# FoX queries and keys projected token-major and turned by DMA, with runs of 32 tokens, and conditioning columns listed and paced anew

## The chip, the cores and the metric

The program runs on one core of a Trainium2 chip. The metric is the device time of one execution in microseconds (us); lower is better. Besides the time there is one profiled execution, with every instruction's start and end on each engine: PE (TensorE matmuls), PEld (its weight loads), DVE (VectorE), ACT (ScalarE), POOL (GpSimd) and SP (which here only issues DMAs).

## The reference

Two decoder layers over 256 tokens of width 2048, float32. Each layer is a token mixer and a SwiGLU feed-forward (FFN), both behind an RMS norm whose scale and shift, as well as the gate of the residual, come from a conditioning vector `c` through `ada_w` (six vectors of 2048 for a layer). Layer 0 mixes with an mLSTM, layer 1 with "forgetting attention" (FoX):

```python
cs = silu(c)
for layer in range(2):
    sh1, sc1, g1, sh2, sc2, g2 = split(cs @ ada_w[layer] + ada_b[layer], 6)
    h = rms_norm(x, norm_mix_w[layer]) * (1 + sc1) + sh1
    y = mlstm_mixer(h, ...) if layer == 0 else fox_mixer(h, ...)
    x = x + g1 * y
    h = rms_norm(x, norm_ffn_w[layer]) * (1 + sc2) + sh2
    g, u = split(h @ w_gate_up[layer], 2)            # 2048 -> 2 * 5632
    x = x + g2 * ((silu(g) * u) @ w_down[layer])     # 5632 -> 2048
return rms_norm(x, final_norm_w)

def fox_mixer(h, w_in, b_f, w_out):                  # 16 heads of 128
    q, k, v, fl = split(h @ w_in, [D, 2 * D, 3 * D])
    cum = cumsum(log_sigmoid(fl + b_f), over tokens)
    s = q @ k.T * 128 ** -0.5 + cum[t] - cum[s]      # for each head, causal
    return (softmax(s) @ v) @ w_out
```

## The kernel before

Every big product is computed in three matmuls from two parts of each operand: a weight tile of 1 MB (`raw`, four slices k of 128 rows, 512 columns) is fetched by SP, ACT rounds it to `hi` (L261), DVE subtracts to get `lo` (L262), and PE multiplies. The activations stand transposed, hidden units on partitions: `hT[:, k]` holds 256 tokens as high parts and then the same 256 as low parts; `y` and `acts` are kept alike.

There are two forms of a column group (512 columns, 16 slices k, four ticks of four slices).

- `group_a` holds the activations still (128 tokens) and streams the weights: for each k and each half of the tokens, high x hi, high x lo and low x hi, three matmuls of 512 columns (L288, L289, L290). Two banks take the result, tokens on partitions ("token-major").
- `group_b` holds the weights still and streams the activations: for each k and each of four blocks of 128 columns, hi against 512 (both parts of the 256 tokens; L271) and lo against 256 (L274). Four banks take the result, columns on partitions; `total` adds the two halves of a bank (ACT L368, DVE L370 or L372).

FoX's q and k need columns of a head on partitions, so `keep_t` makes them with `group_b`, eight column groups in turn: q and k of heads 0 to 3, 4 to 7, 8 to 11 and 12 to 15. All else goes through `group_a`. Where a token-major result has to be turned, PE does it (`turned`), or, in three of the four FFN halves, DVE and DMAs: `blocks` transposes blocks of 32x32 (L353) and writes them to DRAM (`aside`), `gather` reads them back with the partitions in order (L361), both on POOL's queue, and some ticks later `flip` copies from there (ACT L1171, DVE L1172). There the four blocks of 128 columns lie next to each other for each token, so the flip reads with a step of four elements.

A `tick` stands at the end of every four slices: it takes `adv` entries off a list of small steps (`steps`) and pays `rate` of a conditioning column. The heads are such steps: `scores` (L691, L696 and L1229 on PE, then DVE, ACT and DVE), `flip` (PE transposes L958, ACT), `mix` (L1261, L1264, ACT, DVE). A conditioning column is 128 outputs of `cs @ ada_w`: a fetch of 1 MB and one DVE multiply with a sum (L193). They are listed by `want` in the order in which they are computed, 192 in all; `need` makes those at once that a later stage finds missing. When the two gates g1 and g2 of a layer are complete, `grow` spreads them over all partitions (PE, ACT, then POOL's queue).

`bridge` leads from one stage to the next: it ends a residual (DVE L442, L443), forms the norm (ACT, DVE L487), turns it on PE (L498) and begins the next product. Its order on PE, DVE and ACT is written out by hand. Elsewhere the order of each engine's instructions is set when the program is built, by a scheduler that works on estimates; a buffer goes to whoever can have it first. Weights and conditioning columns share five buffers of 1 MB; there are four pairs of `hi` and `lo`, each for two slices, and 16 `slot`s of 512 KB.

Of the kernel before, what the change touches and what calls it, by code (L numbers as in the profile page):

```python
# [27 lines left out]
    r0=(0.75, 0.7, 0.8, 0.5), fr=0.66, r1=(0.3, 0.3, 0.3, 0.3))  # L28
# [3 lines left out]
def kernel(  # L32
# [211 lines left out]

    def tick(n, adv=1):
        drain(adv)
        grow_all()
        bg(n)
# [20 lines left out]
    def mm_b(ps, hi, lo, rhs, first, last):  # L269
        def big():  # L270
            nc.tensor.matmul(ps, hi, rhs, start=first, stop=last, skip_group_check=True)  # L271

        def little():
            nc.tensor.matmul(  # L274
                ps[:, T:], lo, rhs[:, :T], start=False, stop=False, skip_group_check=True
            )

        if last:
            little()
            big()  # L280
        else:
            big()
            little()

# [10 lines left out]

    def group_b(w, nk, c0, act, evac, bgn, adv=1):
        banks = [bank() for _ in range(4)]
        for k in range(0, nk, 4):
            ws = load_w(w, k, 4, c0)
            for m in range(4):  # L300
                cols = slice(m * P, (m + 1) * P)
                for j, (hi, lo) in enumerate(ws):
                    mm_b(
                        banks[m], hi[:, cols], lo[:, cols], act(k + j), k + j == 0, k + j == nk - 1
                    )
                if k + 4 == nk:
                    evac(m, banks[m])
            tick(bgn, adv)
# [43 lines left out]
    def blocks(dst, src, aside):  # L352
        nc.vector.transpose(  # L353
            dst.rearrange("p (j b m) -> p j m b", j=4, m=4),
# [4 lines left out]
    def gather(whole, aside):  # L359
        for j in range(4):  # L360
            nc.gpsimd.dma_start(  # L361
                whole[32 * j : 32 * j + 32].rearrange("a (g b) m -> a g (b m)", b=32),
# [3 lines left out]
    def total(ps, out, scale=None):  # L366
        b = t256()
        nc.scalar.activation(b, ps[:, T:], AF.Copy, scale=1.0 if scale is None else scale)  # L368
        if scale is None:
            nc.vector.tensor_tensor(out, ps[:, :T], b, op=ALU.add)  # L370
        else:
            nc.vector.scalar_tensor_tensor(  # L372
                out=out, in0=ps[:, :T], scalar=scale, in1=b, op0=ALU.mult, op1=ALU.add
            )
# [678 lines left out]

# [57 lines left out]
    def ffn(layer, begun, norm, rates, nsplit=0, srate=0.0, nxt=None):  # L1111
# [23 lines left out]
        if nsplit:  # L1135
            want(0, G2)
            want(1, SC1, SH1)
            want(1, G1)

        rate = rates[0]  # L1140

        def column(c0):
# [280 lines left out]
```

## Time and profile before

| | |
|---|---|
| time, median of 3 runs (lowest, highest) | 2282.02 us (2279.60, 2283.16) |
| time of the profiled execution, and its span | 2279.4 us, 2277.6 us |
| busy share of the span: PE, PEld, DVE, ACT, POOL | 99%, 81%, 73%, 50%, 3% |
| read from HBM, written | 628.44 MB, 10.52 MB; 281 GB/s over the span |
| granted clock of PE, mean | 0.999 |

A row of a group reads: line, engine, operation, output<-inputs, shapes, count | busy us, mean ns of one | idle time of the engine just before them and what ended it. A row of the timeline or of the chain begins with its start and its length in us. A row of a window gives the stretch, its length, then busy us and, in brackets, the count of instructions for each engine. The stages in the span: mLSTM and norm up to 435 us, the first FFN to 1143, FoX from 1143 to 1545 (its q and k columns from 1215 to 1316 and from 1346 to 1444, its output product to 1545), the second FFN to the end. Matmuls overlap in the pipeline, so their pace is read from starts, not from lengths.

### The profile page before, as it was taken

The numbers are of one execution on the slowest core, as the hardware profiler recorded it, in microseconds if no ns is written. First come the engines' busy times: TensorE is split into PE (matmuls) and PEld (weight loads), VectorE is DVE, ScalarE is ACT, GpSimd is POOL, SyncE is SP. The second block draws the span as 40 slices with busy tenths as digits, with TensorE's granted clock in tenths as the row PEclk, the third lists the DMA queues.
The fourth block names the chain that finished last, engine by engine and source line by source line (L and its number), as shares of the span: only waits on it lengthen the run. The fifth ranks groups of instructions, "written<-read, shape, count | busy, mean of one in ns | idle before, by whom it ended". The sixth has DMA issues, their size and how long they took to land.

```text
span 2277.6 us, 26530 instructions
## 1 busy us (share of the span) xinstructions
PE 2255.0 (99%) x10250; PEld 1848.2 (81%) x10250; DVE 1653.0 (73%) x1865; ACT 1139.6 (50%) x1493; POOL 71.2 (3%) x136
## 2 busy tenths in 40 slices
PE   8999999999999999999999999999999999999998
PEld 5877878888888888888888888887888888888886
DVE  7998789878887878875687777777665555555564
ACT  4778564555543344444555444455444443444443
POOL 1000000000000000100000000000100100010000
PEclk9999999999999999999999999999999999999999
DMA  9998989788888889996667877675777665566662
GB/s 394 371 369 321 353 307 354 283 338 334 325 335 330 326 335 349 360 350 219 217 238 288 299 273 277 250 274 189 271 276 255 221 204 189 201 223 219 206 233 98
DMA packets 93571, 640.69 MB, mean 281 GB/s; under 512 B 11443, under 2 KB 11891, under 8 KB 19077
## 3 DMA queue, kind: packets, MB, share of 16 engines
q1 hardware_dynamic: 86400, 617.79, 73.5%
q0 software_dynamic: 6896, 21.08, 3.1%
q8 instruction: 80, 1.31, 0.2%
q14 instruction: 47, 0.38, 0.0%
q10 hardware_dynamic: 148, 0.14, 0.0%
HBM read 628.44 MB, written 10.52 MB: 281 GB/s over the span
## 4 chain that ended last, share of the span: by engine, by line
PE 87%; DVE 5%; DMA 4%; ACT 2%; issue 1%; POOL 0%; SPq 0%; ACTq 0%; DVEq 0%; POOLq 0%
PE mm L289 25%; PE mm L290 25%; PE mm L288 25%; PE mm L271 5%; PE mm L274 3%; DMA ada<-in_ada_w_dram 3%; DVE lo L262 2%; DVE ada L193 2%; ACT hi L261 1%; DMA slot<-in_w_in_dram 1%; PE aux L1010 0%; PE aux L498 0%; PE aux L1229 0%; PE mm L569 0%; PE mm L565 0%
## 5 line engine op out<-in xcount | busy, mean ns | idle before, releaser
L262 DVE TENSOR_TENSOR lo<-raw,hi 128x1024 fp32r<-128x1024 f32 x764 | 924.2, 1221 | 470.8 <-ACT hi L261 469.5
L261 ACT CAST hi<-raw 128x1024 fp32r<-128x1024 f32 x764 | 796.9, 1054 | 870.7 <-PE mm L290 742.2
L289 PE MATMUL mm<-lo,hT 128*128 128x512 f32 x1846 | 720.3, 390 | 3.3 <-DVE lo L262 3.2
L290 PE MATMUL mm<-hi,hT 128*128 128x512 f32 x1846 | 719.8, 390 | 0.0
L288 PE MATMUL mm<-hi,hT 128*128 128x512 f32 x1846 | 719.1, 392 | 0.0
L193 DVE SCALAR_TENSOR_TENSOR ada<-ada,cs 128x2048 f32<-128x2048 f32 x192 | 438.7, 2285 | 55.7 <-DMA ada<-in_ada_w_dram 55.3
L289 PEld LDWEIGHTS mm<-lo,hT 128*128 128x128 f32 x1846 | 346.7, 188 | 78.5 <-DVE lo L262 7.4
L290 PEld LDWEIGHTS mm<-hi,hT 128*128 128x128 f32 x1846 | 346.5, 188 | 72.4 <-issue 0.5
L288 PEld LDWEIGHTS mm<-hi,hT 128*128 128x128 f32 x1846 | 346.5, 188 | 71.9 <-issue 0.5
L288 PE MATMUL mm<-hi,slot 128*128 128x512 f32 x960 | 375.0, 391 | 0.2 <-ACT slot L1043 0.2
L289 PE MATMUL mm<-lo,slot 128*128 128x512 f32 x960 | 374.2, 390 | 0.2 <-DVE lo L262 0.2
L290 PE MATMUL mm<-hi,slot 128*128 128x512 f32 x960 | 374.1, 390 | 0.0
L288 PEld LDWEIGHTS mm<-hi,slot 128*128 128x128 f32 x960 | 180.3, 188 | 38.0 <-ACT slot L1043 0.8
L290 PEld LDWEIGHTS mm<-hi,slot 128*128 128x128 f32 x960 | 180.2, 188 | 37.7 <-issue 0.7
L289 PEld LDWEIGHTS mm<-lo,slot 128*128 128x128 f32 x960 | 180.2, 188 | 37.5 <-DVE lo L262 0.6
L271 PE MATMUL mm<-hT,hi 128*128 128x512 f32 x512 | 181.5, 401 | 0.0
L274 PE MATMUL mm<-hT,lo 128*128 128x256 f32 x512 | 138.4, 281 | 0.4 <-DVE lo L262 0.4
L271 PEld LDWEIGHTS mm<-hT,hi 128*128 128x128 f32 x512 | 94.4, 188 | 19.6
L274 PEld LDWEIGHTS mm<-hT,lo 128*128 128x128 f32 x512 | 96.6, 189 | 4.1 <-DVE lo L262 1.1
L865 ACT ACTIVATE slot<-mm 128x512 f32<-128x512 f32 x78 | 45.3, 596 | 39.7 <-PE mm L290 37.9
L357 POOL DMA_DIRECT2D aside<-t x32 | 18.0, 562 | 1239.7 <-DVE t L353 1239.7
L1172 DVE TENSOR_TENSOR slot<-slot,slot 128x512 fp32r<-128x512 f32 x32 | 34.8, 1090 | 24.8 <-ACT slot L1171 24.8
(220 smaller groups left out, 1049.6 us busy)
## 6 DMA issues: line engine op xcount, KB each, us to landing
ada<-in_ada_w_dram SPq DMA_DIRECT2D x192, 1024.0 KB, 6.3
raw<-in_gate_up_dram SPq DMA_DIRECT2D x176, 1024.0 KB, 5.2
raw<-in_down_dram SPq DMA_DIRECT2D x88, 1024.0 KB, 4.9
raw<-in_fox_in_dram SPq DMA_DIRECT2D x48, 1024.0 KB, 4.9
raw<-in_w_in_dram SPq DMA_DIRECT2D x44, 1024.0 KB, 7.2
raw<-in_w_out_dram SPq DMA_DIRECT2D x16, 1024.0 KB, 5.8
raw<-in_fox_out_dram SPq DMA_DIRECT2D x16, 1024.0 KB, 4.9
aside<-t POOLq DMA_DIRECT2D x32, 256.0 KB, 2.5
```

Source lines behind the costliest of these rows:

```text
L193: nc.vector.scalar_tensor_tensor(out=raw, in0=raw, scalar=1.0, in1=cs, op0=ALU.mult, op1=ALU.mult, accum_out=acc[layer][:, j : j + 1],)
L261: nc.scalar.copy(hi, raw[:, j : j + 2, :])
L262: nc.vector.tensor_tensor(lo, raw[:, j : j + 2, :], hi.bitcast(F32), op=ALU.subtract)
L271: nc.tensor.matmul(ps, hi, rhs, start=first, stop=last, skip_group_check=True)
L274: nc.tensor.matmul(ps[:, T:], lo, rhs[:, :T], start=False, stop=False, skip_group_check=True)
L288: nc.tensor.matmul(ps, a, hi, start=first, stop=False, skip_group_check=True)
L289: nc.tensor.matmul(ps, a, lo, start=False, stop=False, skip_group_check=True)
L290: nc.tensor.matmul(ps, b, hi, start=False, stop=last, skip_group_check=True)
L357: nc.gpsimd.dma_start(aside, dst)
L865: nc.scalar.activation(SP[i][:, t, :], banks[t], func)
L1172: nc.vector.tensor_tensor(dst[:, :, T:], ps, dst[:, :, :T].bitcast(F32), op=ALU.subtract)
```

## The change

Five edits.

- `keep_t` for layer 1 computes q and k with `group_a`, copies the two banks out with ACT (scaled), and turns them with `blocks` and `gather`. The heads' scores read k where `gather` put it; q is copied once more (`begin`, four heads in one ACT copy), six ticks after k's column (four for the last group), and the heads' steps are listed one tick later by `timed`. Two heads run together: scores of both, flips of both, mixes of both, one kind for each tick, since `adv` is 2. The v column that stood before the third group of heads stands behind the fourth.
- `blocks`, `gather` and `tiles` lay a turned tile out in runs of 32 tokens instead of single elements, for the FFN's flips as well.
- Layer 1's `project_out` computes 12 of the 16 slices of its first two columns before the last heads' results are asked for.
- The columns of layer 1 for SC2, SH2 and G2 are listed behind those of layer 0, with G1 after SC2 and SH2.
- The rates are 0.65, 0.6 and 0.52 for the second half of the first FFN (gate and up, then down) and for FoX, instead of 0.8, 0.5 and 0.66. SP's queue now has 9 conditioning columns within the second down product of layer 0 instead of none, 24 instead of 30 within FoX's input columns, and 6 instead of 8 within its output product.

```diff
@@ -25,7 +25,7 @@
 NEG = -1e30
 QN = (6, 9)
 CFG = dict(first=4, pace=(1.0, 1.0, 1.0), n2=4, lr=(0.9, 0.9, 0.95, 1.0, 1.15), sr=0.95, nsplit=11,
-    r0=(0.75, 0.7, 0.8, 0.5), fr=0.66, r1=(0.3, 0.3, 0.3, 0.3))
+    r0=(0.75, 0.7, 0.65, 0.6), fr=0.52, r1=(0.3, 0.3, 0.3, 0.3))
 
 
 @with_exitstack
@@ -242,7 +242,13 @@
         for _ in range(len(steps) if n is None else min(n, len(steps))):
             steps.pop(0)()
 
+    clock = [0]
+    timed = []
+
     def tick(n, adv=1):
+        clock[0] += 1
+        while timed and timed[0][0] <= clock[0]:
+            timed.pop(0)[1]()
         drain(adv)
         grow_all()
         bg(n)
...
@@ -351,7 +327,7 @@
 
     def blocks(dst, src, aside):
         nc.vector.transpose(
-            dst.rearrange("p (j b m) -> p j m b", j=4, m=4),
+            dst.rearrange("p (j m b) -> p j m b", j=4, m=4),
             src.rearrange("p (m j b) -> p j m b", m=4, j=4),
         )
         nc.gpsimd.dma_start(aside, dst)
@@ -359,19 +335,12 @@
     def gather(whole, aside):
         for j in range(4):
             nc.gpsimd.dma_start(
-                whole[32 * j : 32 * j + 32].rearrange("a (g b) m -> a g (b m)", b=32),
+                whole[32 * j : 32 * j + 32].rearrange("a (g c) -> a g c", c=P),
                 aside.rearrange("t (i a) c -> a (t i) c", a=32)[:, :, j * P : (j + 1) * P],
             )
 
...
+    def tiles(whole):
+        return whole.rearrange("p (g m b) -> p m g b", m=4, b=32)
 
     def split_act(src, dst):
         nc.scalar.copy(dst[:, :T], src)
@@ -1051,6 +1020,8 @@
     def interleave(*lists):
         return [f for fs in zip(*lists) for f in fs]
 
+    LAND = 6
+
     def keep_t(c0, bgn, scale=None, adv=1, layer_w=0):
         if layer_w == 0:
             i = COLS.index(c0)
@@ -1064,9 +1035,15 @@
 
             steps.append(flip)
             return o
-        o = slot().rearrange("p (k t) -> p k t", t=T)
-        group_b(w, KT, c0, h_act, lambda m, ps: total(ps, o[:, m, :], scale), bgn, adv)
-        return o
+        banks = group_a(w, c0, h_act, bgn, adv)
+        whole = slot()
+        aside = dram.tile([2, P, 512], F32, tag="aside", name=nm("aside"))
+        for t in range(2):
+            own = t512()
+            nc.scalar.activation(own, banks[t], AF.Copy, scale=1.0 if scale is None else scale)
+            blocks(t512(), own, aside[t])
+        gather(whole, aside)
+        return tiles(whole)
 
     for i in range(1, 4):
         unit(i, start[i], KT, LR[0])
@@ -1092,9 +1069,16 @@
 
     def project_out(wo, res, bgn, adv, upto, norm, w2, heads):
         act = lambda k: act_tile(y, k)
+        first = {}
+        if upto == 12:
+            for i in range(2):
+                first[i] = group_a(wo, 512 * i, act, bgn, adv, kb=upto, more=True)
+            assert not timed
+            drain()
         for i in range(3):
             res.both(i, group_a(
-                wo, 512 * i, act, bgn, adv, before=lambda k: drain() if k >= upto else None
+                wo, 512 * i, act, bgn, adv, ka=upto if i in first else 0, banks=first.get(i),
+                before=lambda k: drain() if k >= upto else None,
             ))
         return bridge(wo, 0, KT, 1536, act, res, 3, norm, w2, heads)
 
@@ -1135,7 +1119,9 @@
         if nsplit:
             want(0, G2)
             want(1, SC1, SH1)
+            want(1, SC2, SH2)
             want(1, G1)
+            want(1, G2)
 
         rate = rates[0]
 
@@ -1156,7 +1142,7 @@
             first = len(acts)
             acts.extend([None, None])
             if lag:
-                whole = slot().rearrange("p (t m) -> p t m", m=4)
+                whole = slot()
                 aside = dram.tile([2, P, 512], F32, tag="aside", name=nm("aside"))
                 for t in range(2):
                     blocks(t512(), sg[:, t, :], aside[t])
@@ -1164,14 +1150,14 @@
 
             def flip(i):
                 acts[first + i] = dst = new_act()
+                hi, lo = dst[:, :, :T], dst[:, :, T:]
                 if lag:
-                    ps = whole[:, :, 2 * i : 2 * i + 2].rearrange("p t m -> p m t")
+                    ps = tiles(whole)[:, 2 * i : 2 * i + 2]
+                    hi, lo = (x.rearrange("p m (g b) -> p m g b", b=32) for x in (hi, lo))
                 else:
                     ps = turned(sg, i)
-                nc.scalar.copy(dst[:, :, :T], ps)
-                nc.vector.tensor_tensor(
-                    dst[:, :, T:], ps, dst[:, :, :T].bitcast(F32), op=ALU.subtract
-                )
+                nc.scalar.copy(hi, ps)
+                nc.vector.tensor_tensor(lo, ps, hi.bitcast(F32), op=ALU.subtract)
 
             steps.extend([lambda: None] * lag)
             steps.extend([lambda: flip(0), lambda: flip(1)])
@@ -1211,8 +1197,6 @@
 
 
     w = fox_in
-    want(1, SC2, SH2)
-    want(1, G2)
     f_raw = slot()[:, : KT * 16].rearrange("p (k c) -> p k c", c=16)
     nc.scalar.dma_start(f_raw, fox_gates)
     y = [None] * 8
@@ -1227,7 +1211,8 @@
             for t in range(2):
                 n = P * (t + 1)
                 nc.tensor.matmul(
-                    S[:, T * t : T * t + n], q[:, t * P : (t + 1) * P], k[:, :n],
+                    S[:, T * t : T * t + n].rearrange("p (g b) -> p g b", b=32),
+                    q[:, t * P : (t + 1) * P], k[:, : n // 32],
                     start=False, stop=t == 1, skip_group_check=True,
                 )
             mx = small([P, 2], "den", bufs=4)
@@ -1292,15 +1277,22 @@
     u3 = split3(cum, 16, new)
     for i in range(4):
         if i == 1:
-            vals[2] = keep_v(group_a(w, 2 * D + 1024, h_act, FR, ka=12, banks=begun[2 * D + 1024]))
-        if i == 2:
-            vals[3] = keep_v(group_a(w, 2 * D + 1536, h_act, FR, 2))
-        q = keep_t(512 * i, FR, P ** -0.5, layer_w=1)
-        k = keep_t(D + 512 * i, FR, layer_w=1)
-        drain()
-        steps.extend(interleave(*[
-            fox_head(4 * i + j, q[:, j, :], k[:, j, :]) for j in range(4)
-        ]))
+            vals[2] = keep_v(
+                group_a(w, 2 * D + 1024, h_act, FR, 2, ka=12, banks=begun[2 * D + 1024])
+            )
+        far = keep_t(512 * i, FR, P ** -0.5, 2, layer_w=1)
+        k = keep_t(D + 512 * i, FR, None, 2, layer_w=1)
+        q = slot().rearrange("p (m t) -> p m t", t=T)
+        heads = [fox_head(4 * i + j, q[:, j, :], k[:, j]) for j in range(4)]
+
+        def begin(q=q, far=far, heads=heads):
+            nc.scalar.copy(q.rearrange("p m (g b) -> p m g b", b=32), far)
+            timed.append((clock[0] + 1, lambda: steps.extend(
+                interleave(*heads[:2]) + interleave(*heads[2:])
+            )))
+
+        timed.append((clock[0] + (LAND if i < 3 else LAND - 2), begin))
+    vals[3] = keep_v(group_a(w, 2 * D + 1536, h_act, FR, 2))
     res = Residual(1, G1, True)
     norm = Norm(res, 1, SC2, SH2)
     begun = project_out(fox_out, res, FR, 2, 12, norm, gate_up[1], [0, DFF, 512])
```

The parts left out remove `mm_b`, `group_b` and `total`, which the kernel no longer calls; the kernel before shows them.

PE where the first heads' scores stand between the matmuls of a column (`sel` and `identb` bring in the forget gates and the mask; `aux` is a bank of scores). Before:

```order
5294 L290 MATMUL mm_8800<-hi_9656,hT 128x512
5295 L691 LDWEIGHTS sel
5296 L691 MATMUL aux_9684<-u_1692_9255,sel 128x512
5297 L696 LDWEIGHTS identb
5298 L696 MATMUL aux_9684<-mask,identb 128x2x128
5299 L1229 MATMUL aux_9684<-slot_9456,slot_9264 128x128
5300 L1229 MATMUL aux_9684<-slot_9456,slot_9264 128x256
5301 L271 MATMUL mm_9708<-hT,hi_9714 128x512
```

With the change:

```order
5382 L660 LDWEIGHTS sel
5383 L660 MATMUL aux_9870<-u_1693_9268,sel 128x512
5384 L665 LDWEIGHTS identb
5385 L665 MATMUL aux_9870<-mask,identb 128x2x128
5386 L1213 MATMUL aux_9870<-slot_9582,slot_9598 128x128
5387 L1213 MATMUL aux_9870<-slot_9582,slot_9598 128x256
5388 L660 LDWEIGHTS sel
5389 L660 MATMUL aux_9885<-u_1693_9268,sel 128x512
5390 L665 LDWEIGHTS identb
5391 L665 MATMUL aux_9885<-mask,identb 128x2x128
5392 L1213 MATMUL aux_9885<-slot_9582,slot_9598 128x128
5393 L1213 MATMUL aux_9885<-slot_9582,slot_9598 128x256
```

One head stood between two columns' matmuls; now two heads stand together, the matmuls around them are those of `group_a`, and 24 of these follow before the two flips.

DVE from the first reduction of a pair's scores to the end of its softmax (`lo` a split for PE, `ada` a conditioning column). Before, heads 4 and 5, one of the two places where two heads ran in one tick:

```order
998 L1239 TENSOR_REDUCE den_10221<-aux_10216 128x1 x2
999 L262 TENSOR_TENSOR lo_10320<-raw_10313,hi_10319 128x1024
1000 L1248 RECIPROCAL r_10223<-r_10223 128x2
1001 L1239 TENSOR_REDUCE den_10236<-aux_10231 128x1
1002 L1251 TENSOR_SCALAR slot_10222<-slot_10222,r_10223 128x128
1003 L1251 TENSOR_SCALAR slot_10222<-slot_10222,r_10223 128x256
1004 L1239 TENSOR_REDUCE den_10236<-aux_10231 128x1
1005 L193 SCALAR_TENSOR_TENSOR ada_10512,acc_125<-ada_10512,cs 128x2048
1006 L1248 RECIPROCAL r_10238<-r_10238 128x2
1007 L262 TENSOR_TENSOR lo_10363<-raw_10360,hi_10362 128x1024
1008 L1251 TENSOR_SCALAR slot_10237<-slot_10237,r_10238 128x128
1009 L1251 TENSOR_SCALAR slot_10237<-slot_10237,r_10238 128x256
```

With the change, heads 2 and 3:

```order
985 L1224 TENSOR_REDUCE den_10054<-aux_10049 128x1 x2
986 L268 TENSOR_TENSOR lo_10133<-raw_10126,hi_10132 128x1024
987 L1233 RECIPROCAL r_10056<-r_10056 128x2
988 L1224 TENSOR_REDUCE den_10069<-aux_10064 128x1
989 L1236 TENSOR_SCALAR slot_10055<-slot_10055,r_10056 128x128
990 L1236 TENSOR_SCALAR slot_10055<-slot_10055,r_10056 128x256
991 L1224 TENSOR_REDUCE den_10069<-aux_10064 128x1
992 L193 SCALAR_TENSOR_TENSOR ada_10295,acc_125<-ada_10295,cs 128x2048
993 L1233 RECIPROCAL r_10071<-r_10071 128x2
994 L268 TENSOR_TENSOR lo_10174<-raw_10171,hi_10173 128x1024
995 L1236 TENSOR_SCALAR slot_10070<-slot_10070,r_10071 128x128
996 L1236 TENSOR_SCALAR slot_10070<-slot_10070,r_10071 128x256
```

The order is the same; four of the eight pairs have an `ada` row in it now (heads 2 and 3, 6 and 7, 8 and 9, 10 and 11), four have none. The flips come one tick after the scores instead of two.

SP's queue at the bridge behind FoX's output product. Before:

```order
453 L252 DMA raw_11972<-in_gate_up_dram 128x2048
454 L252 DMA raw_11974<-in_gate_up_dram 128x2048
455 L252 DMA raw_12165<-in_gate_up_dram 128x2048
456 L252 DMA raw_12226<-in_gate_up_dram 128x2048
457 L252 DMA raw_12274<-in_gate_up_dram 128x2048
458 L192 DMA ada_12321<-in_ada_w_dram 128x2048
459 L252 DMA raw_12324<-in_gate_up_dram 128x2048
```

With the change:

```order
453 L258 DMA raw_11732<-in_gate_up_dram 128x2048
454 L258 DMA raw_11734<-in_gate_up_dram 128x2048
455 L258 DMA raw_11925<-in_gate_up_dram 128x2048
456 L258 DMA raw_11986<-in_gate_up_dram 128x2048
457 L192 DMA ada_12034<-in_ada_w_dram 128x2048
458 L258 DMA raw_12037<-in_gate_up_dram 128x2048
```

The conditioning column stands one fetch sooner. Its buffer was that of `raw_11952`, whose last reader on DVE is the fifth row below; with the change it is that of `raw_11734`, whose last reader is the first row of the piece behind it. DVE there, before:

```order
1178 L262 TENSOR_TENSOR lo_11957<-raw_11952,hi_11956 128x1024
1179 L262 TENSOR_TENSOR slot_11989<-raw_11974,slot_11988 128x1024
1180 L459 TENSOR_REDUCE part_11995<-ss_11309 128x2
1181 L463 TENSOR_SCALAR sbias_11997<-part_11995 128x2
1182 L262 TENSOR_TENSOR lo_11961<-raw_11952,hi_11960 128x1024
1183 L262 TENSOR_TENSOR lo_11965<-raw_11954,hi_11964 128x1024
1184 L262 TENSOR_TENSOR lo_11969<-raw_11954,hi_11968 128x1024
1185 L193 SCALAR_TENSOR_TENSOR ada_12321,acc_125<-ada_12321,cs 128x2048
```

and with the change:

```order
1165 L268 TENSOR_TENSOR slot_11749<-raw_11734,slot_11748 128x1024
1166 L428 TENSOR_REDUCE part_11755<-ss_11076 128x2
1167 L432 TENSOR_SCALAR sbias_11757<-part_11755 128x2
1168 L268 TENSOR_TENSOR lo_11721<-raw_11712,hi_11720 128x1024
1169 L268 TENSOR_TENSOR lo_11725<-raw_11714,hi_11724 128x1024
1170 L268 TENSOR_TENSOR lo_11729<-raw_11714,hi_11728 128x1024
1171 L193 SCALAR_TENSOR_TENSOR ada_12034,acc_125<-ada_12034,cs 128x2048
```

The buffer comes free by the split at the head of this piece, whose like before is row 1179, three DVE instructions ahead of row 1182.

More of the change, by code (lines that the diff above doesn't have):

```diff
@@ L267, in load_w @@
         return [p for j in range(0, nk, 2) for p in split(raw, j)]
[L269 to L275, printed above, removed]
-            )
[L278 to L283, printed above, removed]
     def mm_t(ps, hi, lo, act, t, first, last):
@@ L294, in mm_a @@
             mm_t(ps[t], hi, lo, act, t, first, last)
[L296 to L308, printed above, removed]
     late = []
@@ L361, in gather @@
             nc.gpsimd.dma_start(
-                whole[32 * j : 32 * j + 32].rearrange("a (g b) m -> a g (b m)", b=32),
+                whole[32 * j : 32 * j + 32].rearrange("a (g c) -> a g c", c=P),
                 aside.rearrange("t (i a) c -> a (t i) c", a=32)[:, :, j * P : (j + 1) * P],
             )
[L366 to L374, printed above, removed]
+    def tiles(whole):
+        return whole.rearrange("p (g m b) -> p m g b", m=4, b=32)
     def split_act(src, dst):
@@ L1166, in flip @@
                 acts[first + i] = dst = new_act()
+                hi, lo = dst[:, :, :T], dst[:, :, T:]
                 if lag:
-                    ps = whole[:, :, 2 * i : 2 * i + 2].rearrange("p t m -> p m t")
+                    ps = tiles(whole)[:, 2 * i : 2 * i + 2]
+                    hi, lo = (x.rearrange("p m (g b) -> p m g b", b=32) for x in (hi, lo))
                 else:
                     ps = turned(sg, i)
-                nc.scalar.copy(dst[:, :, :T], ps)
-                nc.vector.tensor_tensor(
-                    dst[:, :, T:], ps, dst[:, :, :T].bitcast(F32), op=ALU.subtract
-                )
+                nc.scalar.copy(hi, ps)
+                nc.vector.tensor_tensor(lo, ps, hi.bitcast(F32), op=ALU.subtract)
             steps.extend([lambda: None] * lag)
```

## The prediction

> **What bounds the kernel now.** I read the busy shares first, then the chain of work that ended last, then PE's pace from starts.
>
> ```profile
> span 2277.6 us, 26530 instructions
> ...
> PE 2255.0 (99%) x10250; PEld 1848.2 (81%) x10250; DVE 1653.0 (73%) x1865; ACT 1139.6 (50%) x1493; POOL 71.2 (3%) x136
> ...
> PE 87%; DVE 5%; DMA 4%; ACT 2%; issue 1%; POOL 0%; SPq 0%; ACTq 0%; DVEq 0%; POOLq 0%
> PE mm L289 25%; PE mm L290 25%; PE mm L288 25%; PE mm L271 5%; PE mm L274 3%; DMA ada<-in_ada_w_dram 3%; DVE lo L262 2%; DVE ada L193 2%; ACT hi L261 1%; DMA slot<-in_w_in_dram 1%; PE aux L1010 0%; PE aux L498 0%; PE aux L1229 0%; PE mm L569 0%; PE mm L565 0%
> ```
>
> PE holds 87% of the chain, and the other engines have room. A busy PE may still be slow, since matmuls overlap; so I take two stretches in which PE does nothing but column groups, and count (PE alone: stretch, length, busy us and count, clock, DMA share, GB/s).
>
> ```profile
> 1590.00:1740.00 150.00, 150.00 (x663) 1.00 0.79 274
> 1216.00:1248.00 32.00, 32.00 (x184) 1.00 0.72 263
> ```
>
> The first is `group_a` in the second FFN: 150.00/663 = 0.226 us for a matmul of 512 columns, 0.227 with two of them counted off as cut at the edges. The second is `group_b` in FoX: 32.00/182 = 0.176 on average over one matmul of 512 and one of 256, so 0.352 for a pair. So PE runs at a fixed pace per matmul, and only fewer or cheaper matmuls, or fewer stops, shorten the kernel. What DVE, ACT and POOL save counts where PE stops for them.
>
> **The column groups of q and k.** Old: 64 pairs, 64 x 0.352 = 22.5 us. New: 96 matmuls of 512, 96 x 0.227 = 21.8. Less by 0.7. A second reading takes q and k of the first four heads, which nothing interrupts: first matmul of the one, and first matmul after the other.
>
> ```profile
> 1215.15 0.39 PE L271 MATMUL mm<-hT,hi 128*128 128x512 f32 x1
> ...
> 1261.23 0.40 PE L288 MATMUL mm<-hi,hT 128*128 128x512 f32 x1
> ```
>
> That is 46.08 us for two columns. In it stand two waits for DVE:
>
> ```profile
> 1246.24 2.29 DVE L193 SCALAR_TENSOR_TENSOR ada<-ada,cs 128x2048 f32<-128x2048 f32 x1 [3.62 <-DMA ada<-in_ada_w_dram]
> ...
> 1249.73 0.39 PE L274 MATMUL mm<-hT,lo 128*128 128x256 f32 x1 [0.27 <-DVE lo L262]
> ...
> 1250.87 0.38 PE L274 MATMUL mm<-hT,lo 128*128 128x256 f32 x1 [0.16 <-DVE lo L262]
> ```
>
> DVE stood 3.62 us before a conditioning column whose data had not landed, and the splits behind it came late: 0.4 us of PE. Without them a column takes (46.08 - 0.43)/2 = 22.8, 1.0 more than the new form. I take 0.9 between the readings, so for eight columns **-7.2 us** (ends -5.6 and -8.8). The two waits I count as gone (**-0.4**; ends 0 and -0.4): with 24 columns in this stage instead of 30 DVE has less in front of its splits. If that cover fails, the next late thing is the same split, at the same price.
>
> The Trainium skill's page "TensorE: Matmul & The Clock Gate", section "Back-to-back issue gap", has the gap as N/2.4 + 2.5 ns: 215.8 ns for 512 columns, 109.2 for 256. By that an old column would be 64 x 325.0 ns = 20.8 us and a new one 20.7, and the eight would give 0.7 us instead of 7.2. The trace does not agree: 0.227 and 0.352 - 0.227 = 0.125.
>
> **What turns q and k.** Durations, from the groups of instructions:
>
> ```profile
> L193 DVE SCALAR_TENSOR_TENSOR ada<-ada,cs 128x2048 f32<-128x2048 f32 x192 | 438.7, 2285 | 55.7 <-DMA ada<-in_ada_w_dram 55.3
> ...
> L865 ACT ACTIVATE slot<-mm 128x512 f32<-128x512 f32 x78 | 45.3, 596 | 39.7 <-PE mm L290 37.9
> ...
> L1171 ACT CAST slot<-slot 128x512 fp32r<-128x512 f32 x32 | 35.7, 1118 | 19.9 <-DMA slot<-aside 19.9
> ...
> L353 DVE STREAM_TRANSPOSE t<-slot 128x512 f32<-128x512 f32 x32 | 31.8, 1066 | 0.0
> ...
> L1229 PE MATMUL aux<-slot,slot 128*128 128x128 f32 (+1 forms) x64 | 13.1, 327 | 0.0
> ...
> L368 ACT ACTIVATE t<-mm 128x256 f32<-128x256 f32 x32 | 12.2, 383 | 17.5 <-PE mm L271 17.5
> ...
> L1171 ACT CAST slot<-aux 128x512 fp32r<-128x512 f32 x12 | 6.9, 583 | 2.0 <-PE aux L346 2.0
> L370 DVE TENSOR_TENSOR slot<-mm,t 128x256 f32<-128x256 f32 x16 | 6.5, 419 | 2.5 <-ACT t L368 2.5
> ```
>
> For each column DVE loses four sums of 0.42 (1.68 us) and gains two transposes of at most 1.07 (2.13): +0.45, or about -0.6 if a transpose into runs takes half, as the flip's ACT copy does without the step of four (583 against 1118). ACT loses 4 x 0.38 and gains 2 x 0.60, and one copy of q for two columns, 1.1 to 2.2 us. DVE's conditioning work there falls by 6 x 2.29 = 14 us. All of this lies beside PE; I cost it at nothing, and the cover is the four pairs of `hi` and `lo` that stand ahead of PE. The shorter flips of the FFN (L1171, L1172) lie beside PE too.
>
> POOL gains two writes and four reads of DRAM for each column. The one flip in the FFN that came late shows how long such a turn lasts; its chain:
>
> ```profile
> 1813.19 1.06 DVE t L353
> ...
> 1814.54 4.05 DMA aside<-t
> ...
> 1819.15 1.76 POOL slot L361 x3
> ...
> 1822.32 7.91 DMA slot<-aside
> 1830.26 1.11 ACT slot L1171
> ```
>
> From the last transpose to the flip 17.1 us, and the first transpose 1 us sooner: 18. The heads' scores come seven ticks after k's column, five for the last group: 5 x 24 x 0.227 = 27.2 us of matmuls beside the heads' own. With 3 us for the two copies out (1.2) and for DVE to come to the transposes, the last group has 6 us to spare. PE's cost: 0. If it is late, ACT's copy of q or PE's scores wait, and behind ACT's copy the next `hi`. On POOL's queue the spreading of layer 1's g1 now stands behind the last group's reads; its first user is the residual of FoX's output product, over six ticks on, and a turn of the same kind fits there: 0.
>
> Scores now read k in runs of 32 with gaps. The trace has no such matmul. Bounds: 0, and the whole of L1229 once more, 13.1 us. I take 0: 583 against 1118 is the price of a step of four elements, and runs of 32 are nearer to reading without a step.
>
> **Two heads in a tick, flips one tick later.** Heads 4 and 5 did the same before, with one conditioning column between (PE's first matmul of the scores, its first one after them, and DVE):
>
> ```profile
> 1324.84 0.39 PE L691 MATMUL aux<-u,sel 96*128 96x512 bf16 x1
> ...
> 1326.64 0.58 PE L288 MATMUL mm<-hi,hT 128*128 128x512 f32 x1
> ...
> 1328.79 2.28 DVE L193 SCALAR_TENSOR_TENSOR ada<-ada,cs 128x2048 f32<-128x2048 f32 x1
> ...
> 1332.19 0.54 DVE L1251 TENSOR_SCALAR slot<-slot,r 128x128 f32<-128x128 f32 x2
> ```
>
> Softmax of the second head ends 1332.73 - 1324.84 = 7.9 us after the scores begin. PE now has 1.8 + 24 x 0.227 = 7.25 us before the first flip, and the first head's flip before the second's. The wait is at most 0.65 in the four pairs with a column between, nothing in the others (7.9 - 2.3 = 5.6). I take 0.3 x 4: **+1.2** (ends 0 and, with one more multiply before every pair's end, 8 x (0.65 + 2.28) = +23).
>
> **The bridge behind FoX.** The chain, and PE's gap there:
>
> ```profile
> 1530.05 1.24 DVE lo L262
> 1531.30 7.02 DMA ada<-in_ada_w_dram
> 1538.42 2.30 DVE ada L193 x2
> ```
>
> ```profile
> 1542.03 0.39 PE L290 MATMUL mm<-hi,slot 128*128 128x512 f32 x1
> 1543.99 1.06 PE L498 MATMUL aux<-ident,slot 128*128 128x128 f32 x8 [1.58 <-DVE slot L487]
> ```
>
> A conditioning column stands ahead of the residual on DVE, and its fetch waited for a buffer until 1531.3; PE stopped for 1543.99 - 1542.03 - 0.23 = 1.7 us. With the change its buffer comes free by the split whose like ended here:
>
> ```profile
> 1527.98 1.22 DVE L262 TENSOR_TENSOR slot<-raw,slot 128x1024 fp32r<-128x1024 f32 x1
> ```
>
> That is 1529.2, 2.1 us sooner, more than PE's stop: **-1.7** (ends 0 and -1.7).
>
> The 12 slices that `project_out` now takes ahead change no matmul; the page names no wait of PE for the last heads' results, so they cost and gain 0, and the last pair has six ticks' matmuls beside it.
>
> **The late flip.**
>
> ```profile
> 1833.68 0.50 PE L289 MATMUL mm<-lo,slot 128*128 128x512 f32 x1 [0.18 <-DVE lo L262]
> ```
>
> Copies of half the length make up 0.5 us each: **-0.2**. The columns listed anew and the rates change no sum of work, 192 multiplies either way; in the second half of the first FFN PE is never without weights for longer than these stops, so they cost 0 (-1 to +2, the stop at the bridge behind FoX taken once either way).
>
> Sum: -7.2 - 0.4 + 1.2 - 1.7 - 0.2 = -8.3. The profiled execution took 2279.4 us, of which 1.8 lie outside its span; it would take 2271.1. The median of the three runs lies 2.6 above it, so I forecast 2282.0 - 8.3 = 2273.7, about 2274.
>
> **Rivals.** *No gain in the columns.* If a matmul of 256 columns took just half of one of 512, a pair would take 1.5 x 0.227 = 0.3405 and 64 of them 21.8 us, a new column's time. Then only the stops count, -0.4 + 1.2 - 1.7 - 0.2 = -1.1: 2281. For it: half the columns stream through in half the time. Against it: both readings above, though the reading by uninterrupted columns could hold stops too small for the trace to name. The Trainium skill's rule of the gap, quoted above, comes out near this rival.
>
> *PE waits for the softmax of every pair.* If DVE is behind when a pair begins, as at 1246, its chain ends one multiply later, and PE waits up to 2.9 us eight times: -9.5 + 23 = +14, 2296. It turns the forecast over from 9.5/8 = 1.2 us a pair on. For it: five or so instructions between, in fixed order. Against it: less conditioning work in the stage, and four pairs without a column between.
>
> *Scores at half pace.* -8.3 + 13.1 = +4.8: 2287. For it: ACT's doubled time with a step. Against it: the run's length.
>
> **How the numbers follow.** The forecast 0.72, no gain 0.16, the waits 0.07, the half pace 0.05. A measurement of this kernel can tell about 0.2%, 4.6 us, from no change. Faster: 0.72; same: 0.16; slower: 0.12. The range leaves out both slower rivals (0.12) and some tail: low 2270 (all ends together, -8.8 - 0.4 - 1.7 - 0.2 = -11.1, and a little for the runs' spread), high 2283 (no gain, and the runs' spread above it).
>
> **What would show it.** Uninterrupted q and k columns at 21.8 us, with L271 and L274 gone. Transposes nearer 0.55 than 1.07 us and flips near 0.6. No wait of PE for the turned k, less than 0.65 us at a second flip, none at the bridge behind FoX. The forecast is wrong if the stage from 1215 to 1544 shrinks by less than 5 us, or if what it gains is lost in the second half of the first FFN, where conditioning columns now stand.

## The result, and the profile after

The changed kernel takes 2306.38 us (median of 4 runs, 2302.92 to 2311.61), the kernel before beside it 2281.05 us (4 runs, 2279.60 to 2283.16): ratio 1.0119, 95% interval 1.0101 to 1.0136. It is 1.2% slower; I forecast 2274, 0.4% faster. The profiled execution took 2311.61 us, the longest of the four, so its stretches are a few us long.

The page of the changed kernel: span, busy shares, the chain that ended last by engine and by line.

```profile
span 2309.8 us, 26147 instructions
...
PE 2262.9 (98%) x9994; PEld 1843.4 (80%) x9994; DVE 1628.5 (71%) x1849; ACT 1127.4 (49%) x1481; POOL 98.9 (4%) x184
...
PE 77%; DMA 10%; DVE 7%; issue 4%; ACT 2%; POOL 0%; DVEq 0%; SPq 0%; ACTq 0%
PE mm L279 24%; PE mm L280 24%; PE mm L278 24%; DMA ada<-in_ada_w_dram 9%; DVE lo L268 3%; DVE ada L193 2%; ACT hi L267 1%; DMA slot<-in_w_in_dram 1%; PE aux L467 0%; PE aux L979 0%; DMA slot<-aside 0%; PE mm L538 0%; PE mm L534 0%; PE mm L535 0%; PE aux L322 0%
```

PE has 256 matmuls less and takes longer, and the fetch of conditioning columns holds 9% of the chain instead of 3%. The groups of instructions show what became of the new work:

```profile
L279 PE MATMUL mm<-lo,hT 128*128 128x512 f32 x2102 | 823.6, 392 | 10.6 <-DVE lo L268 10.5
L193 DVE SCALAR_TENSOR_TENSOR ada<-ada,cs 128x2048 f32<-128x2048 f32 x192 | 439.0, 2286 | 132.9 <-DMA ada<-in_ada_w_dram 132.6
L329 DVE STREAM_TRANSPOSE t<-slot 128x512 f32<-128x512 f32 x32 | 20.7, 685 | 0.0
L1159 ACT CAST slot<-slot 128x512 fp32r<-128x512 f32 x32 | 19.7, 620 | 22.1 <-DMA slot<-aside 22.1
L1213 PE MATMUL aux<-slot,slot 128*128 128x128 f32 (+1 forms) x64 | 13.1, 327 | 0.0
L927 PE MATMUL aux<-ident,slot 128*128 128x128 f32 x60 | 11.0, 300 | 10.7 <-DVE slot L1236 10.7
```

Every price of an instruction came out at or near my figure: transposes 0.685 us, flips 0.620, scores 0.327 as before, with no wait for k. What has grown are waits: DVE for conditioning fetches (132.6 us, before 55.3), PE for `lo`, PE's head flips for the softmax.

Where the time went, by starts in the traces (us; from the first silu of the first FFN's sixth group to the last multiply of its last residual, and from there to the last multiply of FoX's last residual):

| | FFN, second half | FoX | span |
|---|---|---|---|
| before | 483.0 | 398.5 | 2277.6 |
| changed | 495.1 | 417.6 | 2309.8 |

So 12 us were lost in the first FFN and 19 in FoX, where I expected to win all 8. Everything else is within 1.5 us.

The largest stop in FoX, in the timelines of DVE, SP, POOL and PE and in the windows (stretch, length, busy us and count of PE, PEld, DVE, ACT, POOL, clock, DMA share, GB/s):

```profile
1280.55 4.62 DVE L268 TENSOR_TENSOR lo<-raw,hi 128x1024 fp32r<-128x1024 f32 x4
1295.70 2.29 DVE L193 SCALAR_TENSOR_TENSOR ada<-ada,cs 128x2048 f32<-128x2048 f32 x1 [10.52 <-DMA ada<-in_ada_w_dram]
```

```profile
1282.93 0.33 SPq L192 DMA_DIRECT2D ada<-in_ada_w_dram  x1
```

```profile
1281.99 2.34 POOL L337 DMA_DIRECT2D slot<-aside  x4 [6.65 <-DMA aside<-t]
```

```profile
1293.31 0.39 PE L278 MATMUL mm<-hi,hT 128*128 128x512 f32 x1
1299.19 0.79 PE L279 MATMUL mm<-lo,hT 128*128 128x512 f32 x1 [5.49 <-DVE lo L268]
```

```profile
1285.00:1290.00 5.00, 5.00 (x24) 4.14 (x23) 0.17 (x1) 2.11 (x2) 0.00 (x0) 1.00 1.00 259
1290.00:1295.00 5.00, 3.70 (x17) 2.73 (x15) 0.00 (x0) 2.10 (x2) 0.00 (x0) 1.00 0.86 261
1295.00:1300.00 5.00, 0.81 (x2) 0.72 (x3) 4.30 (x4) 0.00 (x0) 0.00 (x0) 0.64 0.21 54
1300.00:1305.00 5.00, 5.00 (x16) 3.90 (x16) 2.62 (x4) 1.05 (x1) 0.00 (x0) 0.68 1.00 421
```

Read them together. DVE has split all it may (four pairs ahead of PE) by 1285.2 and comes to a conditioning multiply whose fetch SP issued only 2.2 us sooner, at 1282.93. The four reads of k's turn were issued a microsecond before, at 1281.99. The DMA engines are full (share 1.00), the fetch lands after 12.7 us, and DVE, which keeps its order, stands 10.5 us. PE meanwhile uses up the four pairs and stops for 5.6 us (from 1293.31 to 1299.19 are 5.88 us between two starts, instead of 0.23). In the two windows from 1295 to 1305 the granted clock is 0.64 and 0.68, and behind the stop 16 matmuls stand in 5 us instead of 24.

What the turns did to the fetches shows in the DMA issues between 1225 and 1500 us (median us to landing at the end of a row), of before and then of the changed kernel:

```profile
raw<-in_fox_in_dram SPq DMA_DIRECT2D x31, 1024.0 KB, 4.8
ada<-in_ada_w_dram SPq DMA_DIRECT2D x28, 1024.0 KB, 4.9
```

```profile
q0 software_dynamic: 3136, 9.45, 11.5%
raw<-in_fox_in_dram SPq DMA_DIRECT2D x32, 1024.0 KB, 6.2
ada<-in_ada_w_dram SPq DMA_DIRECT2D x21, 1024.0 KB, 7.2
```

POOL's queue (q0) took 11.5% of the engines there, and a conditioning fetch landed after 7.2 instead of 4.9 us. In both kernels DVE came to a multiply about 5 us after its fetch was issued (from the issue to the end of DVE's instruction ahead of the multiply, a fetch's lead: median 4.7 before, 5.0 after). Before, that was nearly enough; now it isn't. DVE's waits in FoX (us in total, times, longest), of before and then of the changed kernel:

```profile
DVE ada L193 <- DMA ada<-in_ada_w_dram: 28.3, 21, 3.9
DVE ada L193 <- DMA ada<-in_ada_w_dram: 60.9, 19, 10.5
```

### The profile page after: what moved, and what is told of

Read it like the earlier page. It is cut to its first block, busy times and chain, and to the rows that moved or that the text cites. A ratio compares the mean times of both kernels' runs of the same rounds, so it can differ in the third digit from the quotient of the medians.

```text
span 2309.8 us, 26147 instructions
## 1 busy us (share of the span) xinstructions
PE 2262.9 (98%) x9994; PEld 1843.4 (80%) x9994; DVE 1628.5 (71%) x1849; ACT 1127.4 (49%) x1481; POOL 98.9 (4%) x184
## 4 chain that ended last, share of the span: by engine, by line
PE 77%; DMA 10%; DVE 7%; issue 4%; ACT 2%; POOL 0%; DVEq 0%; SPq 0%; ACTq 0%
PE mm L279 24%; PE mm L280 24%; PE mm L278 24%; DMA ada<-in_ada_w_dram 9%; DVE lo L268 3%; DVE ada L193 2%; ACT hi L267 1%; DMA slot<-in_w_in_dram 1%; PE aux L467 0%; PE aux L979 0%; DMA slot<-aside 0%; PE mm L538 0%; PE mm L534 0%; PE mm L535 0%; PE aux L322 0%
## 5 line engine op out<-in xcount | busy, mean ns | idle before, releaser
L279 PE MATMUL mm<-lo,hT 128*128 128x512 f32 x2102 | 823.6, 392 | 10.6 <-DVE lo L268 10.5
L278 PE MATMUL mm<-hi,hT 128*128 128x512 f32 x2102 | 823.1, 393 | 0.0
L280 PE MATMUL mm<-hi,hT 128*128 128x512 f32 x2102 | 822.2, 391 | 0.0
L193 DVE SCALAR_TENSOR_TENSOR ada<-ada,cs 128x2048 f32<-128x2048 f32 x192 | 439.0, 2286 | 132.9 <-DMA ada<-in_ada_w_dram 132.6
L279 PEld LDWEIGHTS mm<-lo,hT 128*128 128x128 f32 x2102 | 396.5, 189 | 97.4 <-DVE lo L268 16.2
L280 PEld LDWEIGHTS mm<-hi,hT 128*128 128x128 f32 x2102 | 396.3, 189 | 82.7 <-issue 0.5
L278 PEld LDWEIGHTS mm<-hi,hT 128*128 128x128 f32 x2102 | 396.2, 189 | 82.0 <-issue 0.5
L333 POOL DMA_DIRECT2D aside<-t x48 | 27.0, 563 | 1170.4 <-DVE t L329 1169.6
L834 ACT ACTIVATE slot<-mm 128x512 f32<-128x512 f32 x78 | 45.2, 596 | 39.7 <-PE mm L280 37.9
L337 POOL DMA_DIRECT2D slot<-aside x96 | 56.2, 592 | 130.9 <-DMA aside<-t 76.3
L1160 DVE TENSOR_TENSOR slot<-slot,slot 128x512 fp32r<-128x512 f32 x32 | 21.9, 688 | 24.7 <-ACT slot L1159 24.6
L417 ACT ACTIVATE t<-X 128x512 f32<-128x512 f32 x32 | 20.2, 630 | 36.0 <-DVE X L412 36.0
L1138 ACT ACTIVATE slot<-mm 128x512 f32<-128x512 f32 x44 | 25.6, 599 | 15.1 <-PE mm L280 14.8
L412 DVE TENSOR_TENSOR X<-X,t 128x512 f32<-128x512 f32 x48 | 32.3, 686 | 0.5
```

Of the source, the lines that this page charges most:

```text
L193: nc.vector.scalar_tensor_tensor(out=raw, in0=raw, scalar=1.0, in1=cs, op0=ALU.mult, op1=ALU.mult, accum_out=acc[layer][:, j : j + 1],)
L278: nc.tensor.matmul(ps, a, hi, start=first, stop=False, skip_group_check=True)
L279: nc.tensor.matmul(ps, a, lo, start=False, stop=False, skip_group_check=True)
L280: nc.tensor.matmul(ps, b, hi, start=False, stop=last, skip_group_check=True)
L333: nc.gpsimd.dma_start(aside, dst)
L337: nc.gpsimd.dma_start(whole[32 * j : 32 * j + 32].rearrange("a (g c) -> a g c", c=P), aside.rearrange("t (i a) c -> a (t i) c", a=32)[:, : ...
```

## Experiments

Theory A was formed from this: *late conditioning fetches hold DVE, which keeps its order, and `lo` comes late; the turns delay the fetches in FoX, and the new rates bring the fetches to where they are late in the FFN.* The rivals are named in the expectations. Ratios are to the kernel before on the same chip.

### One part of the change at a time

`listing`: the kernel before with the new listing and rates.

```diff
-    r0=(0.75, 0.7, 0.8, 0.5), fr=0.66, ...
+    r0=(0.75, 0.7, 0.65, 0.6), fr=0.52, ...
             want(1, SC1, SH1)
+            want(1, SC2, SH2)
             want(1, G1)
+            want(1, G2)
...
-    want(1, SC2, SH2)
-    want(1, G2)
```

> The kernel before with only the new listing and the new rates of the conditioning columns (0.65, 0.6 and 0.52 for 0.8, 0.5 and 0.66); q and k still by group_b. Theory A (transfers collide): a conditioning fetch that lands late holds DVE, and the split behind it; in the second half of the first FFN this happens beside the FFN's own turn by DMA, which both kernels have, once columns stand in that stretch. Then the stretch from the first to the second block of the FFN to the bridge loses about 12 us as in the changed kernel, and the whole comes to 2291 to 2294. Theory B (the listing costs nothing, all of the loss comes with the q and k turns): 2281 to 2283.

Measured 2294.61 us, ratio 1.0061 (1.0045 to 1.0077). Second half of the FFN 501.8 us (+18.9), FoX 396.0 (-2.4). The time is just above theory A's 2291 to 2294, and the FFN loses more than its 12 us. Theory B falls: the listing alone costs over half of the loss, all of it in the FFN. Its largest stop is of another sort than FoX's; ACT and then the windows:

```profile
1071.72 2.10 ACT L1173 CAST slot<-slot 128x512 fp32r<-128x512 f32 x2 [12.51 <-DMA slot<-aside]
```

```profile
1070.00:1075.00 5.00, 0.17 (x1) 0.18 (x1) 2.16 (x3) 3.28 (x4) 0.00 (x0) 0.91 0.11 39
1075.00:1080.00 5.00, 2.29 (x5) 1.49 (x6) 5.00 (x5) 2.61 (x3) 0.00 (x0) 0.50 0.35 100
```

Here the turn is the one that lands late, and ACT, in order too, stands 12.5 us before the flip with the `hi` of the next weights behind it.

`runs32`: the kernel before with `blocks`, `gather`, `tiles` and the FFN's flips of the changed kernel, nothing else.

```diff
-            dst.rearrange("p (j b m) -> p j m b", j=4, m=4),
+            dst.rearrange("p (j m b) -> p j m b", j=4, m=4),
...
-                whole[32 * j : 32 * j + 32].rearrange("a (g b) m -> a g (b m)", b=32),
+                whole[32 * j : 32 * j + 32].rearrange("a (g c) -> a g c", c=P),
...
-                    ps = whole[:, :, 2 * i : 2 * i + 2].rearrange("p t m -> p m t")
+                    ps = tiles(whole)[:, 2 * i : 2 * i + 2]
```

> The kernel before with only the layout in runs of 32 tokens, in the turns of the FFN. Theory A: nothing but the late flip at 1833, 2281.8; within 2279 to 2284. Theory C (reading in runs of 32 is slow somewhere, in the gather or in PE's reads): the FFN's turns show it, over 2285.

Measured 2279.78, ratio 0.9998 (0.9988 to 1.0008): the layout costs nothing, and gains nothing that can be told. Theory C falls.

`old_listing`: the changed kernel with the listing and rates of before (the diff of `listing`, turned round).

> The changed kernel with the old listing and the old rates. Theory A: the first FFN has its 12 us back, FoX has 0.66 instead of 0.52 conditioning columns a tick beside the turns of q and k and loses as much as in the changed kernel (19 us) or up to 10 more: 2294 to 2304. Theory D (the listing alone loses everything): 2274, my forecast. Theory B: 2306 or above.

Measured 2296.59, ratio 1.0067 (1.0042 to 1.0091): FFN 485.2 (+2.3), FoX 413.4 (+14.9). Theory D falls. There are two losses, one for each part of the change. They do not simply add up: 15.0 (`listing`) and 17.0 make 32 us, the change as a whole lost 25. And FoX lost less here than in the changed kernel, where theory A had as much or more.

`pe_turn`: q and k turned by PE.

```diff
-            blocks(t512(), own, aside[t])
-        gather(whole, aside)
-        return tiles(whole)
+        def turn():
+            for i in range(2):
+                nc.scalar.copy(whole[:, 2 * i : 2 * i + 2, :], turned(own, i))
+        timed.append((clock[0] + 2, turn))
```

> The changed kernel, but q and k are turned by PE (64 transposes of 128x128 more, by 0.109 us 7 us) and not by DVE, DRAM and the gather; heads and ticks as in the changed kernel, the scores read q and k without a step. Theory A: the stops of PE in FoX go, the loss in the first FFN stays: 2306 - 19 - 8 + 7 = 2286. Theory E (two heads in a tick, the flips one tick later, or the longer wait for the softmax lose the time): the stops stay, 2306 + 7 = 2313.

Measured 2293.44, ratio 1.0058 (1.0042 to 1.0075): FFN 494.3, FoX 400.7, which is 17 us less than in the changed kernel although PE has 64 transposes more. Theory E falls. It is 7 us above my 2286. DVE's waits for fetches have not all gone (15.5 us in FoX), and the 19 us that I took off came from the longest run of the changed kernel; how much each explains is not shown. The landing is back with the turns gone (1225 to 1500 us):

```profile
ada<-in_ada_w_dram SPq DMA_DIRECT2D x23, 1024.0 KB, 5.0
```

### The wait itself

In the changed kernel a conditioning multiply stands on DVE ahead of splits of weights that were fetched before it (in the piece of DVE's order with the change, `ada_10295` stands ahead of `lo_10174`). `multiply_later` ties it to data: its scalar 1.0 is made from the last `lo` of the weight tile fetched next, from the second half of the first FFN on.

```diff
     def load_w(w, k0, nk, c0):
+        due = list(owed)
         raw = fetch(w, k0, nk, c0)
-        return [p for j in range(0, nk, 2) for p in split(raw, j)]
+        pairs = [p for j in range(0, nk, 2) for p in split(raw, j)]
+        for multiply in due:
+            ...
+            one = small([P, 1], "one", bufs=4)
+            nc.vector.tensor_scalar(
+                one, pairs[-1][1][:, :1].bitcast(F32), 0.0, 1.0, op0=ALU.mult, op1=ALU.add
+            )
+            multiply(one)
+        return pairs
```

> The changed kernel, but from the second half of the first FFN on each conditioning multiply is tied to the last `lo` of the weight tile that is fetched next (its scalar 1.0 is made from that `lo` by a small DVE instruction), so that DVE comes to it when its fetch has had one tick more. Theory A (DVE, in order, stands before a conditioning fetch that is not there, and the `lo` splits behind it come late): DVE's wait for ada falls from 132.6 us to under 40, the stops in FoX go (-19, and up to -8 of what I forecast), the stop in the first FFN behind ACT's flip stays: 2281 to 2288. Theory F (the transfers as such are too slow together, weights and turns included): the wait moves to `hi` before its weights, and the time stays above 2298.

Measured 2268.97, ratio 0.9957 (0.9942 to 0.9972): 37 us under the changed kernel, 12 under theory A's range, and faster than the kernel before. DVE's wait for `ada` is 8.6 us. Also the stop at the FFN's flip went, which I had expected to stay: FFN 481.1, FoX 390.0. Why it went was not isolated. The same program once more, as `multiply_later_2`, beside `before_later`:

> multiply_later once more, on the same chip as before_later. Theory A: 2269, 8 to 12 us under before_later. Theory H: within 2 us of before_later.

Measured 2268.73, ratio 0.9950 (0.9937 to 0.9962). Its page, group of multiplies and DMA issues (1225 to 1500 us):

```profile
span 2266.9 us, 26271 instructions
...
PE 92%; DVE 4%; DMA 2%; ACT 1%; issue 1%; SPq 0%; ACTq 0%; DVEq 0%
```

```profile
L195 DVE SCALAR_TENSOR_TENSOR ada<-ada,one,cs 128x2048 f32<-128x2048 f32 x111 | 261.0, 2351 | 3.9
```

```profile
q0 software_dynamic: 3136, 9.45, 11.7%
raw<-in_fox_in_dram SPq DMA_DIRECT2D x32, 1024.0 KB, 6.5
ada<-in_ada_w_dram SPq DMA_DIRECT2D x23, 1024.0 KB, 5.7
```

The turns still take their share of the DMA engines and the weights still land after 6.5 us; theory F (the transfers together are too slow) falls. But DVE now comes to a multiply 21.5 us after the issue (median in FoX; 16.5 in the FFN) instead of 5.0 (5.5 in the FFN), and none of the 111 tied multiplies waits for its fetch.

`before_later`: the kernel before with the tie alone.

> The kernel before with the tie of the conditioning multiplies alone. Theory A: there PE lost under 3 us to late fetches (0.5 near 1250, 1.7 at the bridge), so 2277 to 2281; the gain of multiply_later over the kernel before is then the change's own, with its late multiplies repaired. Theory H (the tie is worth 11 us in any kernel and the change nothing): 2269 to 2271.

Measured 2282.46, ratio 1.0008 (0.9999 to 1.0017); theory H falls. The time is above theory A's 2277 to 2281 too, and `multiply_later_2` is 13.7 us under it, not 8 to 12. FoX gains 2.5 us (396.0; `runs32`, in which nothing of FoX is changed, has 397.2 in its trace, so about half of that is what two traces differ by anyway). But the FFN loses 5.6 (488.6), which theory A had not said. A multiply that comes late holds its buffer, one of the five that the weights use too, and at the old rate of 0.8 ACT waits for weights (800 to 1150 us):

```profile
ACT hi L273 <- DMA raw<-in_gate_up_dram: 57.3, 17, 7.0
```

`multiply_later_2`, with 0.65 there, has five such waits of 13.2 us in all. That these waits cost the 5.6 us is argued, not shown: `old_listing_later` below, with 0.8 as well, has 65.6 us of them in the same stretch and loses 1.2 us in the FFN.

`old_listing_later`: `old_listing` with the tie.

> The changed kernel with the old listing and rates, and with the same tie of the conditioning multiplies. Theory A: no loss in the first FFN, no stops in FoX: 2272 to 2279, faster than the kernel before. Theory F: as old_listing, 2294 to 2298.

Measured 2272.43, ratio 0.9973 (0.9961 to 0.9986); FFN 484.1, FoX 390.0. As theory A had it. It is 3.5 us slower than `multiply_later`, 3.0 of them in the FFN: the new listing and rates do harm without the tie and a little good with it.

### Controls

`no_fetch_fox`: the changed kernel with the fetch of FoX's conditioning columns taken out.

```diff
-        nc.sync.dma_start(raw, ada_w[layer, j])
+        if not dry[0]:
+            nc.sync.dma_start(raw, ada_w[layer, j])
...
-            out=raw, in0=raw, scalar=1.0, in1=cs, ...
+            out=raw, in0=cs if dry[0] else raw, scalar=1.0, in1=cs, ...
```

> The changed kernel without the conditioning fetches in FoX's input columns; their multiplies stay and take `cs` for the fetched columns (that part of the conditioning is left out). Theory A: the stops of PE in FoX go, the flips' wait for the softmax with them; the first FFN keeps its loss: 2279 to 2287. Theory E (the longer chain of two heads in a tick loses the time by itself): 2300 or above.

Measured 2286.41, ratio 1.0025 (1.0013 to 1.0037): FoX 394.3 us, 23 less than with the fetches; the FFN keeps its loss (494.6). Within A's range; three stops of 1.3 us are left in FoX, at two flips of heads and where g1 is spread.

`listing_no_down`: `listing` without columns in the FFN's second down product.

```diff
-    r0=(0.75, 0.7, 0.65, 0.6), fr=0.52, ...
+    r0=(0.75, 0.7, 0.65, 0.0), fr=0.71, ...
```

> The kernel before with the new listing, but no conditioning column within the first FFN's second down product (rates 0.65, 0 and, so that none is missing later, 0.71 in FoX). Theory A: the stop of PE at 1068 in `listing` (6.0 and 3.7 us, and some 3 at a lowered clock) comes from two fetches that were issued together with the reads of the last turn, so that ACT stood before the flip; it goes, and the five smaller ones before it (925 to 1002, 5 us in all) stay: 2294.6 - 12.5 = 2282, up to 2285. Theory G (the rate of 0.65 or the order of the columns is what costs, wherever they stand): 2290 or above.

Measured 2288.06, ratio 1.0034 (1.0021 to 1.0047), between the two ranges. The stop at 1068 is gone (FFN 490.5, against 501.8), the small ones at 932 to 1027 are there (5.4 us in all).

`rate_only`: the same rates with the columns in the old order.

> The kernel before with the old order of the columns, and rates of 0.65, 0 and 0.71 (as in listing_no_down). Theory J (the lower rate leaves DVE with less to do, it comes to each multiply sooner after its fetch was issued, 5.5 us instead of 8): the gate and up columns of the second half lose their 6 us, 2286 to 2288. Theory K (the order of the columns, thus what is read from where, costs): no loss there, 2280 to 2282.

Measured 2286.48, ratio 1.0027 (1.0017 to 1.0036); FFN 487.8. Theory J: the lower rate by itself costs some 5 us, and the order of the columns little (`listing_no_down`, with the new order, is 1.6 us slower). The lead there (667 to 1015 us) has a median of 8.1 to 8.5 us at a rate of 0.8 and of 5.4 to 5.9 at 0.65. The landing did not grow, as the DMA issues show for before and then for the changed kernel:

```profile
ada<-in_ada_w_dram SPq DMA_DIRECT2D x43, 1024.0 KB, 7.2
ada<-in_ada_w_dram SPq DMA_DIRECT2D x42, 1024.0 KB, 6.4
```

So in these columns of the FFN the fetches are late because DVE comes sooner, not because they land later; in FoX it is the other way round. That DVE comes sooner because it has less to do fits this; it wasn't isolated.

`pe_turn_later`: `pe_turn` with the tie.

> The changed kernel with the tie, and q and k turned by PE instead of DMAs. Theory A: no stops in either, PE has 64 transposes of 0.109 us more, 2269 + 7 = 2276. If it is below 2271, the turn by DMA still costs what it saves.

Measured 2277.43, ratio 0.9985 (0.9976 to 0.9995), 8.7 us above `multiply_later_2`; FoX 398.1 against 390.0. With the waits gone, the turn by DMA is worth its 64 transposes.

## Why the prediction was wrong

The step that failed is "What turns q and k": "All of this lies beside PE; I cost it at nothing, and the cover is the four pairs of `hi` and `lo` that stand ahead of PE." I asked whether the turn would be done in time for its own users, and it is. I did not ask what its transfers do to the transfers beside them. I counted POOL's writes and reads as instructions of a queue with room, and not as 11.5% of the DMA engines in a stretch where they were 0.72 busy (1216 to 1248). The cover itself I named and did not measure against the wait: four pairs last PE 8 x 6 x 0.227 = 10.9 us at most, and a wait of 10.5 us together with the multiply (2.3) and the split (1.2) behind it is more. Cost there: 19.1 us and the gain not had.

- **Columns of q and k (-7.2) and flips (+1.2).** Between 1228 and 1276 us the changed kernel shows nothing but column groups:

```profile
1228.00:1276.00 48.00, 48.00 (x213) 39.74 (x212) 35.09 (x41) 25.73 (x31) 4.60 (x8) 1.00 0.80 296
```

  48.00/212 = 0.226, a column of 96 takes 21.7 us, as forecast. An old column without waits takes 22.61 (`before_later`: the first q and k together 45.22, from 1220.44 to 1265.66), a new one at my 0.227 us a matmul 21.79, so eight columns are worth 0.82 x 8 = -6.6. With the tie on both sides (`before_later`, `old_listing_later`) FoX takes 390.0 instead of 396.0. The two terms were right in kind and near in size, once uncovered; that their sum was -6.0 too is luck, since the flips then cost 0 and not 1.2. The end of -8.8 does not follow from the readings given, which reach -8.3.
- **Waits at 1249 and at the bridge (-0.4 and -1.7).** With the tie alone both waits are gone from the trace of the kernel before, and FoX has 2.5 us less, about these two, though not more than twice what two traces differ by. In the changed kernel the bridge's stop is gone, but "If that cover fails, the next late thing is the same split, at the same price" was wrong in its price: the same split, at 5.6 us instead of 0.3.
- **Flips after the softmax.** 10.7 us in five flips in the changed kernel, in `multiply_later_2` 0. The order of two heads in a tick isn't what waits; DVE held by a fetch is (without the fetches, in `no_fetch_fox`, two stops of 1.3 us are left). My rival "PE waits for the softmax of every pair" (2296, 0.07) had DVE behind, but by a multiply's length, not by a landing.
- **"The columns listed anew and the rates change no sum of work ... so they cost 0 (-1 to +2)."** It cost 12.1 us in the profile of the changed kernel, 18.9 alone. Of the 18.9, 11.3 go with the columns in the second down product (`listing_no_down`), beside which the flip's turn lands late. In the gate and up columns I left out the lead of the fetches: 8.1 us before, 5.5 in the changed kernel, with a landing of 6.4. The evidence I gave, that PE was never long without weights there, was taken under the rate that was being changed. I named this place as one that could make me wrong, with no case for it in the range.
- **Turn of the layout, late flip (-0.2), scores (0).** `runs32` shows nothing that can be told from 0, and L1213 has its old 0.327 us.
- **What a stop costs.** I priced stops by their length. After 5.6 us the windows show a granted clock of 0.64; in `listing` 0.50. The Trainium skill has this ("TensorE: Matmul & The Clock Gate", Part 1: after an idle window of about 3.4 us the array runs at half clock until a window is busy). The rows above agree in kind, but not in the length: in `listing` a stop of 2.0 us, from 1002.6 to 1004.6, was followed by a granted clock of 0.50 from 1006 to 1009. In the changed kernel matmuls then stand 0.427 us apart instead of 0.227, which adds 1.0 to 2.4 us behind each of five stops, 7 of the 32 us between the spans.
- **A row I had seen.** The chain of before already had a slow landing beside a turn's reads:

```profile
870.72 12.91 DMA ada<-in_ada_w_dram
```

  PE lost 0.2 us there, and I passed over it; it said that such a landing can take 12.9 us.

What isn't settled: why the stop at the FFN's flip went with the tie, what costs `before_later` its 5.6 us in the FFN, and whether another tie (to the first `lo`, or two tiles on) would do better.

## What to carry to other kernels

Where an engine keeps its order, a transfer that it waits for needs its lead compared with the landing time that the new traffic makes, not with the old one: 5 us of lead against 4.9 of landing had no slack left, which 0.4 us of waits on PE hardly showed. A new rate moves the lead as well, here from 8.1 to 5.5 us. A transfer added beside a stream of fetches is priced by what it does to them. And when a scheduler puts work where it estimates the data, tie the work to something that arrives later; here an instruction of 0.15 us for each of 111 columns turned a change that lost 25 us into one that gains 12.

## What the runs showed of the hardware

- A conditioning fetch of 1 MB took 4.9 us (median) beside weights alone and 7.2 beside the turns' 9.45 MB, 12.7 at the worst in FoX; the turns' own reads took 7.2 us for 128 KB. Not the bytes but the landing made the loss: with the same 9.45 MB and a lead of 21 us there was none.
- Transposes into runs of 32 took 0.685 us against 1.066 into single elements, and ACT's flips 0.620 against 1.118; PE read k in runs of 32 at the old pace (0.327 us). None of it moved the time.
- A multiply with its scalar from a tile takes 2.351 us against 2.284 with a constant (`multiply_later_2`).
- A stop of PE of 2.0 us was enough for 3 us at half clock behind it (`listing`, 1006 to 1009).
